# Rounds of weight sums issued by GpSimd instead of SyncE, and two more raw buffers for the first layer's seven block products

## The chip, the cores and the metric

The kernel runs on one core of one Trainium2 chip. The metric is the device time of one execution, in microseconds (us). The core's engines are TensorE (PE, with its weight loads shown as PEld), VectorE (DVE), ScalarE (ACT), GpSimd (POOL) and SyncE (SP). Each works through its own instructions in program order and waits on semaphores for the others. SP only issues DMAs here, and a DMA that has to wait holds back all that stands behind it on the engine that issues it.

## The reference

The network is a trunk of four residual layers on x of shape (256, 1024), float32: layers 0 and 3 are gated MLPs with a causal mix over positions, layer 1 is a dilated window attention, layer 2 a pooling mixer.

```
for i in range(DEPTH):                       # DEPTH = 4
    kind, j = i % 3, i // 3
    h = rms_norm(x, norm_gain[i])
    if kind == 0:   y = mixer_a(h, a_w_in[j], a_v_gain[j], a_w_s[j], a_b_s[j], a_w_out[j])
    elif kind == 1: y = mixer_b(...)
    else:           y = mixer_c(...)
    x = x + y

def mixer_a(h, w_in, v_gain, w_s, b_s, w_out):        # w_in 1024 x 6144, w_out 2048 x 1024
    u, v, z = three blocks of h @ w_in, 2048 wide each
    v = rms_norm(v, v_gain)
    mixed = causal 128x128 matrices, per group and chunk, applied to v, plus b_s
    return (u * mixed * silu(z)) @ w_out
```

## The kernel before

All matmuls are done in three passes: each float32 operand is split into a high part (ACT copies it to a type that PE reads at full rate, line 94) and a low part (DVE subtracts, line 97), and `mm3` (lines 89 to 91) adds high x high, high x low and low x high in PSUM.

**Weights as a stream of units.** All weights come from DRAM as units of 128 x 1024 float32 (512 KB), in the order in which PE uses them. A unit is loaded into a raw buffer (line 181, issued by SP), split into a pair w..h, w..l (seven pairs), and used. `split_units` keeps the splits five units (`AHEAD`) ahead of the product that is being written out, and `load_free` issues the load of a later unit at the point of the program where the raw buffer that it takes has been split for the last time. `raw_place` says which buffer a unit takes: one of four buffers `wr`, and from layer 3's blocks on one of six, `wr` x 4, `xs` and `wx`.

**Seven products instead of eight.** Four products (the first half of the output product of layer 0, `("wo", 0)`, and three pairs of layer 3, `("zu", 0)`, `("zu", 2)`, `("zu", 3)`) are done as 2 x 2 blocks with seven block products instead of eight. For this, sums of weight blocks and sums of blocks of the left operand are needed. `sums_of_quarters` makes the first kind in 32 rounds of 256 columns (`parts`: eight for each of the four products, in the order of `BLOCKS`). A round loads four quarter pieces into `stage` or into the buffer `xs` (512 KB, line 195), adds them in place with four DVE instructions of 128 x 256 (line 198), and writes four sums to a DRAM buffer `sums...` (512 KB, line 201). The units that hold such sums are later loaded from there. In the trace the rounds in `xs` are named `qswo` and `qszu`. `left_sums` makes the second kind on DVE and ACT (lines 592 to 615); in layer 0 it uses the two halves of `wx` and one more tile as room.

**The order of the work.** The program is written out by generators. `tick` moves a clock in program order, one step for every half unit or so; a generator that yields n goes on n ticks later. So the numbers in `sums_of_quarters` (delay before the first round, `load` ticks between the load and the first add, one tick between adds, `wait` ticks more before the write, four ticks to the next load) place the instructions of a round between the others. The queue of each engine is in that order.

In layer 0 the program writes out v (4 x 4 units), then z and u in turn (8 x 4 units, each u followed by a gating step on DVE, lines 759 and 764, and transposes `yp` on PE), then `proj_seven`: seven block products (`xw`, `yw`, `zw`, `xw`, `zw`, `xw`, `ww`) of 12 matmuls and two units each, units 48 to 61. Every product but the first use of a bank adds to what the bank holds, after DVE has added the bank to x (line 636). Then `proj_out` does the rest of the output product, units 62 to 69 (`wo`), line 560 completes x, and layer 1's norm begins: ms on DVE, a power on POOL (line 306), xs on DVE (line 314), transposes on PE, hT on ACT and DVE.

The rounds before: eight for wo0 and four for zu0 in layer 0 (`PARTS = (8, 4, 8, 8)`: one series of eight in `stage` from tick 8, one of four in `xs` from tick 15), sixteen in layer 1, and four in layer 2. POOL has few instructions besides: constants, the powers, the loads of small tables (lines 668 to 671, 902 to 908, 1172, 1174) and memsets in layer 2.

Of the kernel before, what the change touches and what calls it, by code (L numbers as in the profile page):

```python
# [41 lines left out]
MIX_LAG = 4  # L42
LAST_LAG = 1
LAST_AHEAD = 3
WARM = 17
FILL = 4


BLOCKS = {("wo", 0): 48, ("zu", 0): -48, ("zu", 2): -32, ("zu", 3): -16}
PARTS = (8, 4, 8, 8)  # L50


@with_exitstack
def hybrid_trunk_kernel(ctx, tc, x, wts, norm_gainT, a_v_gain, a_wsT, a_bsT, b_gl, b_gv, c_scaleT,
                        masks, rope, rcnt, out):
    nc = tc.nc
# [9 lines left out]
    wx = cp.tile([P, 2, HALF], F32, name="wx")  # L66
# [39 lines left out]
    def spawn(gen, delay=0):  # L106
        if delay == 0:
            try:
                delay = next(gen)
            except StopIteration:  # L110
                return
        tasks.append([now[0] + delay, gen])
# [34 lines left out]
    sums = {(b, j): dp.tile([4, P, UNIT], F32, name=f"sums{b[0]}{b[1]}{j}") for b in BLOCKS for j in range(2)}  # L147

    def first_of(b):

        return BLOCKS[b] % n_units

    for b in sorted(BLOCKS, key=first_of, reverse=True):
        z = first_of(b)
# [3 lines left out]
    n_seq = len(seq)  # L158

    more_raw = seq.index((("zu", 0), 0, 0))  # L160

    raw_users = {"wr": [-1] * RAW_BUFS, "xs": [-1], "wx": [-1]}

    def raw_place(i):

        return ("wr", "wr", "wr", "wr", "xs", "wx")[(i - more_raw) % 6] if i >= more_raw else "wr"

    def load_free():

# [12 lines left out]
            raws.append(raw)  # L182
            loaded[0] += 1

    def sums_of_quarters(parts, shared=False, delay=0, wait=2, load=7):

        if delay:
            yield delay  # L190
        for b, j, c in parts:
            z = first_of(b) + j
            cs = slice(c * 256, (c + 1) * 256)
            q = cp.tile([P, 4, 256], F32, tag="xs", name=f"qs{b[0]}{b[1]}{j}{c}", bufs=1) if shared else stage
            nc.sync.dma_start(q, wts[z:z + 8:2][:, :, cs].rearrange("i p c -> p i c"))
            yield load
            for a, d in ((0, 2), (2, 3), (3, 0), (1, 3)):
                nc.vector.tensor_tensor(q[:, a], q[:, a], q[:, d], op=ALU.add)  # L198
                yield 1
            yield wait  # L200
            nc.sync.dma_start(sums[b, j][:, :, cs].rearrange("i p c -> p i c"), q)
            yield 4

    def split_hi(n):
# [86 lines left out]

    keep_warm(WARM)

# [291 lines left out]
    def left_sums(name, quarter, place, smh, sml, key, pause=1):  # L585

        def full(k, t):
            d = place(f"sq{name}{k}{t}").rearrange("p (k c) -> p k c", c=P)  # L590
            hh, hl = (a.bitcast(F32) for a in quarter(k, t))
            nc.vector.tensor_tensor(d, hh, hl, op=ALU.add)
            return d

        def parted(i, d):
            hi_of(smh[:, i], d)
            yield pause
            lo_of(sml[:, i], d, smh[:, i])
            yield pause

        a22 = full(1, 1)
        yield pause
        a21 = full(0, 1)
        yield pause
        nc.vector.tensor_tensor(a22, a21, a22, op=ALU.subtract)
        yield from parted(S_A21_A22, a22)
        a11 = full(0, 0)
        yield pause
        nc.vector.tensor_tensor(a21, a11, a21, op=ALU.subtract)
        yield from parted(S_A11_A21, a21)  # L610
        nc.vector.tensor_tensor(a11, a22, a11, op=ALU.subtract)
        yield from parted(S_REST, a11)
        a12 = full(1, 0)
        yield pause
        nc.vector.tensor_tensor(a12, a12, a11, op=ALU.add)
        yield from parted(S_A12_REST, a12)
        done.add(key)
# [13 lines left out]
    def proj_seven(layer, yT, smh, sml):  # L631


        def add(t, n, o, op=ALU.add):
            xh = xt[t][:, n * HALF:(n + 1) * HALF]
            nc.vector.tensor_tensor(xh, xh, o, op=op)
            yield 1

        def quarter(k, t):
            return lambda i: yT(4 * k + i, t)  # L640

        xb = pp(f"xw{layer}")
        part_product(xb, quarter(0, 0), True)
        spawn(add(0, 0, xb), 1)
        yb = pp(f"yw{layer}")
        part_product(yb, quarter(1, 0), True)
        spawn(add(0, 0, yb), 1)
        need(("sums", layer))
        zb = pp(f"zw{layer}")
        part_product(zb, sum_tile(smh, sml, S_A21_A22), True)  # L650
        spawn(add(1, 1, zb), 1)
        part_product(xb, sum_tile(smh, sml, S_REST), False)
        spawn(add(0, 1, xb, ALU.subtract), 1)
        part_product(zb, sum_tile(smh, sml, S_A12_REST), False)
        spawn(add(0, 1, zb), 1)
        part_product(xb, sum_tile(smh, sml, S_A11_A21), False)
        spawn(add(1, 1, xb, ALU.subtract), 1)
        spawn(add(1, 0, xb), 1)
        wb = pp(f"ww{layer}")
        part_product(wb, quarter(1, 1), True)  # L660
        spawn(add(1, 0, wb), 1)
# [16 lines left out]
    def layer_a(layer, consts, pl, mid):  # L678
# [101 lines left out]
        if layer == DEPTH - 1 or ("wo", layer) in BLOCKS:  # L780
            smh, sml = pair(pl, [P, 4, 4, P], "sm", f"sm{layer}", 1)
# [65 lines left out]
        for n in range(4):  # L847
            spawn(v_task(n, first if first and n == 0 else
                         proj_tok(f"v{layer}{n}", skew=layer if n == 0 else None)))
            if layer == 0 and n == 0:  # L850
                spawn(sums_of_quarters(parts[:4] + parts[8:8 + PARTS[1]], False, 8, 1, 6))
                spawn(sums_of_quarters(parts[4:8], True, 15, 1, 6))
            if layer == DEPTH - 1 and n == 0:
                spawn(left_sums(layer, h_quarter, lambda n: tmp("sz", n, 4), smh, sml, ("sums", layer)), 4)
        def get(k, t):
# [4 lines left out]
        def y_sums():  # L860

            while ("y", layer, 1) not in done:
                yield 1
            room = [wx[:, 0], wx[:, 1], tmp("yq", "yq", 1)]
            turns = [0]

            def place(name):
                turns[0] += 1
                return room[(turns[0] - 1) % 3]

            def y_quarter(k, t):
                return (a[:, :, t * P:(t + 1) * P] for a in yT[k])

            yield from left_sums(layer, y_quarter, place, smh, sml, ("sums", layer), 2)

        for n in range(4):
            if n == 2 and ("wo", layer) in BLOCKS:
# [14 lines left out]

        if ("wo", layer) in BLOCKS:
            proj_seven(layer, get, smh, sml)
        proj_out(layer, 16, get, KT if layer == DEPTH - 1 or ("wo", layer) in BLOCKS else 0)


# [21 lines left out]
    def layer_b(layer, consts, pl):  # L919
# [215 lines left out]
        for hp in range(NHEAD // 2):  # L1135
            for g in range(NG):
                spawn(qk_task(hp, g, proj_tok(f"qk{hp}{g}", skew=layer if hp == 0 and g == 0 else None)))
                if hp == 0 and g == 0:
                    n0, n1, n2 = (sum(PARTS[:i]) for i in (2, 3, 4))
                    spawn(sums_of_quarters(parts[n0:n1]))  # L1140
# [28 lines left out]
    def layer_c(layer, pl):  # L1169
# [103 lines left out]

        a, b, c, d = C_ORDER
        spawn(gate_tok(a, proj_tok(f"cz{a}", skew=layer)))
        spawn(sums_of_quarters(parts[sum(PARTS):], wait=8))
        spawn(gate_feat(b, proj_feat(f"cz{b}")))
        spawn(pool_task(a, proj_feat(f"cx{a}")))
        spawn(pool_task(b, proj_feat(f"cx{b}")))
# [19 lines left out]
    parts = [(b, j, c) for b in BLOCKS for j in range(2) for c in range(4)]  # L1299
# [157 lines left out]
```

## Time and profile before

| | |
|---|---|
| median of 3 runs | 841.59 us (839.37 to 841.69) |
| the profiled execution, its own time | 840.14 us |
| its span, first to last instruction | 838.4 us |
| busy PE, DVE, ACT, POOL | 823.8, 640.8, 523.4, 43.8 us |
| mean granted TensorE clock | 0.995 of full speed |
| DMA | 195.75 MB, mean 233 GB/s |

The span and the time of the profiled execution differ by 1.74 us, which lie around the instructions. Busy time of PE is an upper bound: matmuls overlap, and a matmul at half the clock counts as busy too.

### The profile page before, as it was taken

What the parts mean: (1) busy time and instruction counts of PE and PEld (TensorE: products, weight loads), DVE (VectorE), ACT (ScalarE), POOL (GpSimd) and SP (SyncE); (2) the same over time, 40 slices, a digit from 0 to 9 for tenths busy, and PEclk for the clock granted to TensorE, in tenths of its full rate; (3) what the DMA queues carried; (4) which work ended last, traced back from release to release, by engine and by line L of the source; (5) the groups of instructions that cost most, each with busy time, mean ns of one, the idle gap of its engine ahead of it and who ended that gap; (6) DMA issues with size and microseconds to landing.
All of it is one profiled execution on the core that took longest, in us unless ns stands there. A gap on an engine that the chain in (4) does not pass through costs nothing.

```text
span 838.4 us, 12737 instructions
## 1 busy us (share of the span) xinstructions
PE 823.8 (98%) x4573; PEld 710.1 (85%) x4573; DVE 640.8 (76%) x1112; ACT 523.4 (62%) x957; POOL 43.8 (5%) x69
## 2 busy tenths in 40 slices
PE   9999999889999999999999999999999999999998
PEld 7887888668988988988988989999988888788887
DVE  5797788876858768768768676798964799979692
ACT  7675454454858778678678557445643659657570
POOL 1101000000001001001001012000000000000000
PEclk9999999989999999999999999999999999999999
DMA  8889886694796767757656258656696258868661
GB/s 290 308 286 322 295 295 209 232 303 161 268 330 207 224 205 237 235 184 248 224 193 224 86 176 295 213 193 211 211 316 221 97 185 305 306 200 318 213 260 51
DMA packets 79424, 195.75 MB, mean 233 GB/s; under 512 B 6304, under 2 KB 39856, under 8 KB 79232
## 3 DMA queue, kind: packets, MB, share of 16 engines
q1 hardware_dynamic: 78096, 190.86, 67.3%
q0 software_dynamic: 976, 3.79, 1.4%
q8 instruction: 36, 0.59, 0.3%
q10 hardware_dynamic: 288, 0.28, 0.2%
q14 instruction: 28, 0.23, 0.1%
HBM read 177.08 MB, written 17.83 MB: 232 GB/s over the span
## 4 chain that ended last, share of the span: by engine, by line
PE 80%; DVE 8%; DMA 6%; ACT 3%; issue 3%; POOL 0%; ACTq 0%; DVEq 0%
PE qk L91 5%; PE qk L89 5%; PE qk L90 5%; DMA wr<-in_wts_dram 5%; PE wo L89 4%; PE wo L91 4%; PE wo L90 4%; PE v L89 2%; PE v L91 2%; PE v L90 2%; PE cz L91 2%; PE cz L89 2%; PE cz L90 2%; PE cx L89 2%; PE cx L90 2%
## 5 line engine op out<-in xcount | busy, mean ns | idle before, releaser
L198 DVE TENSOR_TENSOR stage<-stage 128x256 f32<-128x256 f32 x80 | 33.5, 419 | 2.4 <-DMA stage<-in_wts_dram 1.9
L942 POOL TENSOR_TENSOR qr<-qm,m 128x8 f32<-128x8 f32 x12 | 20.1, 1675 | 228.7 <-DVE qm L941 228.7
L937 ACT ACTIVATE junk<-qk 128x128 bf16<-128x128 f32 x96 | 26.7, 278 | 7.3 <-PE qk L91 4.6
L946 ACT ACTIVATE qn<-qk,qr 128x128 f32<-128x128 f32 x96 | 27.6, 382 | 3.6 <-POOL qr L942 3.6
L324 ACT ACTIVATE hT<-hp,gT 128x128 fp32r<-128x128 f32 x48 | 13.1, 383 | 14.9 <-PE hp L320 14.9
L560 DVE TENSOR_TENSOR x<-wo,x 128x512 f32<-128x512 f32 (+1 forms) x16 | 10.8, 673 | 13.3 <-PE wo L91 13.3
L941 DVE TENSOR_SCALAR qm<-qs 128x8 f32<-128x8 f32 x12 | 2.1, 172 | 22.1 <-ACT junk L937 22.1
L306 POOL TENSOR_TENSOR r<-ms,m 128x1 f32<-128x1 f32 x6 | 4.3, 710 | 280.6 <-DVE ms L303 280.6
L937 ACT ACTIVATION_READ_ACCUMULATOR junk<-qk 128x1 f32 x96 | 18.8, 196 | 0.0
L329 DVE SCALAR_TENSOR_TENSOR hT<-hp,gT,hT 128x128 fp32r<-128x128 f32 x48 | 13.5, 343 | 6.2 <-ACT hT L324 6.2
L298 ACT ACTIVATE junk<-x 128x512 bf16<-128x512 f32 x16 | 10.2, 638 | 10.1 <-DVE x L560 9.9
L1036 ACT ACTIVATE p<-p,rl 128x384 f32<-128x384 f32 (+1 forms) x16 | 11.5, 769 | 6.1 <-DVE rl L1035 6.1
L967 PE MATMUL qt<-ident,qn 128*128 128x128 f32 x96 | 14.5, 274 | 0.4 <-DVE qk00l L975 0.4
L967 PEld LDWEIGHTS qt<-ident,qn 128*128 128x128 f32 x96 | 11.3, 140 | 3.7 <-issue 1.9
L198 DVE TENSOR_TENSOR qszu<-qszu 128x256 f32<-128x256 f32 x32 | 13.4, 420 | 0.4 <-DMA qszu<-in_wts_dram 0.2
L959 DVE TENSOR_TENSOR rb<-qn,kcb 128x32 f32<-128x32 f32 x96 | 13.7, 183 | 0.0
L1032 ACT ACTIVATE p<-p,nb 128x768 f32<-128x768 f32 x8 | 7.5, 938 | 7.3 <-DVE nb L1031 7.3
L772 PEld LDWEIGHTS yp<-ident,yy 128*128 128x128 f32 x64 | 7.5, 139 | 5.3 <-issue 1.4
L772 PE MATMUL yp<-ident,yy 128*128 128x128 f32 x64 | 9.9, 277 | 2.0 <-DVE yy L764 1.0
L955 DVE TENSOR_TENSOR ra<-qn,kcb 128x64 f32<-128x64 f32 x48 | 10.5, 220 | 0.8
L697 DVE TENSOR_TENSOR vv<-v,kc 128x512 f32<-128x512 f32 x16 | 10.3, 682 | 0.7 <-ACT junk L695 0.7
L759 DVE SCALAR_TENSOR_TENSOR sz<-u,m,sz 128x512 f32<-128x512 f32 x8 | 6.0, 745 | 5.3 <-PE u L91 5.3
(3030 smaller groups left out, 3377.3 us busy)
## 6 DMA issues: line engine op xcount, KB each, us to landing
wr<-in_wts_dram SPq DMA_DIRECT2D x256, 512.0 KB, 4.6
stage<-in_wts_dram SPq DMA_DIRECT2D x20, 512.0 KB, 5.1
wr<-sumszu SPq DMA_DIRECT2D x20, 512.0 KB, 4.6
sumszu<-stage SPq DMA_DIRECT2D x16, 512.0 KB, 6.2
wr<-sumswo SPq DMA_DIRECT2D x8, 512.0 KB, 4.6
qszu<-in_wts_dram SPq DMA_DIRECT2D x8, 512.0 KB, 5.0
sumszu<-qszu SPq DMA_DIRECT2D x8, 512.0 KB, 5.0
wx<-in_wts_dram SPq DMA_DIRECT2D x7, 512.0 KB, 5.6
```

The source lines that it names most:

```text
L89: nc.tensor.matmul(out_ap, lh[0], rh[0], start=start, stop=False, skip_group_check=True)
L90: nc.tensor.matmul(out_ap, lh[0], rh[1], start=False, stop=False, skip_group_check=True)
L91: nc.tensor.matmul(out_ap, lh[1], rh[0], start=False, stop=stop, skip_group_check=True)
L198: nc.vector.tensor_tensor(q[:, a], q[:, a], q[:, d], op=ALU.add)
L324: nc.scalar.activation(h_parts(layer)[0][:, k, t * P:(t + 1) * P], pt[:, k % 4], AF.Copy, scale=gT[:, layer, k:k + 1])
L329: nc.vector.scalar_tensor_tensor(hTl, pt[:, k % 4], gT[:, layer, k:k + 1], hTh.bitcast(F32), op0=ALU.mult, op1=ALU.subtract)
L772: nc.tensor.transpose(pt[:, k], ys[t][:, k * P:(k + 1) * P], ident)
L937: nc.scalar.activation(junk[:, :HD], ov[t][:, h], AF.Square, accum_out=ssq[t][:, h:h + 1])
L942: nc.gpsimd.tensor_tensor(rqs, ms, m05_row[:, :8], op=ALU.pow)
L946: nc.scalar.activation(qn[t][:, h], ov[t][:, h], AF.Copy, scale=rq[t][:, h:h + 1])
L959: nc.vector.tensor_tensor(rb[:, hs, s0:s0 + 16], qn[t][:, hs, s1:s1 + 16], c, op=ALU.mult)
L967: nc.tensor.transpose(pts[t][:, h], qn[t][:, h], ident)
```

## The change

The rounds of layers 0 and 2 are issued by GpSimd (`queue=nc.gpsimd`), loads and writes alike; those of layer 1 stay on SP. Layer 0's eight rounds for wo0 are dealt to `stage` and `xs` in turn (four each, from tick 4 and tick 11). The rounds for zu0 that stood behind them in layer 0 go from four to two, and these two begin after `proj_seven` has been written out. Layer 1 has sixteen rounds as before, layer 2 has six instead of four, each 19 ticks after the last instead of 23. The 14 units of the first layer's seven products take six raw buffers, with `xs` and `wx` at the fifth and sixth place. `left_sums` in layer 0 pauses one tick between its steps instead of two.

```
+MORE = 2
-PARTS = (8, 4, 8, 8)
+PARTS = (8, 2, 8, 8)
...
     more_raw = seq.index((("zu", 0), 0, 0))
+    out_raw = first_of(("wo", 0))
...
     def raw_place(i):
-        return ("wr", "wr", "wr", "wr", "xs", "wx")[(i - more_raw) % 6] if i >= more_raw else "wr"
+        six = i >= more_raw or out_raw <= i < out_raw + 14
+        return ("xs", "wx", "wr", "wr", "wr", "wr")[(i - (more_raw if i >= more_raw else out_raw) + MORE) % 6] if six else "wr"
...
-    def sums_of_quarters(parts, shared=False, delay=0, wait=2, load=7):
+    def sums_of_quarters(parts, shared=False, delay=0, wait=2, load=7, queue=nc.sync):
...
-            nc.sync.dma_start(q, wts[z:z + 8:2][:, :, cs].rearrange("i p c -> p i c"))
+            queue.dma_start(q, wts[z:z + 8:2][:, :, cs].rearrange("i p c -> p i c"))
...
-            nc.sync.dma_start(sums[b, j][:, :, cs].rearrange("i p c -> p i c"), q)
+            queue.dma_start(sums[b, j][:, :, cs].rearrange("i p c -> p i c"), q)
...
-                spawn(sums_of_quarters(parts[:4] + parts[8:8 + PARTS[1]], False, 8, 1, 6))
-                spawn(sums_of_quarters(parts[4:8], True, 15, 1, 6))
+                spawn(sums_of_quarters(parts[0:8:2], False, 4, 1, 6, nc.gpsimd))
+                spawn(sums_of_quarters(parts[1:8:2], True, 11, 1, 6, nc.gpsimd))
...
-            yield from left_sums(layer, y_quarter, place, smh, sml, ("sums", layer), 2)
+            yield from left_sums(layer, y_quarter, place, smh, sml, ("sums", layer))
...
             proj_seven(layer, get, smh, sml)
+            spawn(sums_of_quarters(parts[8:8 + PARTS[1]], False, 0, 1, 5, nc.gpsimd))
...
-        spawn(sums_of_quarters(parts[sum(PARTS):], wait=8))
+        spawn(sums_of_quarters(parts[sum(PARTS):], False, 0, 4, 7, nc.gpsimd))
```

## Rows read from the trace of the kernel before

**Rows 1.** Stretches of 5 us: busy time of each engine, granted clock, DMA share, GB/s

```profile
150.00:155.00 5.00, 5.00 (x26) 4.12 (x24) 4.96 (x9) 2.95 (x4) 0.00 (x0) 1.00 0.14 36
...
180.00:185.00 5.00, 4.97 (x12) 3.90 (x13) 4.81 (x7) 2.81 (x3) 0.00 (x0) 0.50 0.84 261
```

**Rows 2.** Timeline of PE: start, duration, instruction, idle before and its releaser

```profile
78.71 0.74 PE L772 MATMUL yp<-ident,yy 128*128 128x128 f32 x4 [1.02 <-DVE yy L764]
...
149.52 0.39 PE L89 MATMUL xw<-w48h,y00h 128*128 128x512 f32 x1
...
152.24 0.60 PE L772 MATMUL yp<-ident,yy 128*128 128x128 f32 x4
...
156.20 0.66 PE L772 MATMUL yp<-ident,yy 128*128 128x128 f32 x4 [0.59 <-DVE y03l L97]
...
163.56 0.47 PE L89 MATMUL zw<-w56h,sm0h 128*128 128x512 f32 x1 [1.22 <-DVE x L636]
...
166.95 0.47 PE L89 MATMUL xw<-w58h,sm0h 128*128 128x512 f32 x1 [0.42 <-DVE x L636]
...
176.53 0.47 PE L89 MATMUL wo<-w63h,y02h 128*128 128x512 f32 x1 [1.10 <-DVE x L636]
...
180.03 0.79 PE L89 MATMUL wo<-w63h,y02h 128*128 128x512 f32 x1 [2.56 <-DVE x L636]
...
190.12 0.39 PE L89 MATMUL wo<-w66h,y03h 128*128 128x512 f32 x1
```

**Rows 3.** Chain of work that ended last, 140 to 200 us: start, duration, what

```profile
159.37 4.41 DMA wr<-sumswo
```

**Rows 4.** Timeline of SP's DMA issues, merged: start, duration with waits, DMA, count

```profile
145.36 8.74 SPq L181 DMA_DIRECT2D wr<-in_wts_dram  x2
155.24 6.79 SPq L181 DMA_DIRECT2D wr<-sumswo  x4
```

**Rows 5.** Timeline of DVE in the seven products, and one row of 65 us

```profile
65.64 1.22 DVE L97 TENSOR_TENSOR w24l<-wr,w24h 128x1024 fp32r<-128x1024 f32 x1
...
149.04 0.75 DVE L759 SCALAR_TENSOR_TENSOR sz<-u,m,sz 128x512 f32<-128x512 f32 x1 [3.71 <-PE u L91]
...
152.19 0.42 DVE L198 TENSOR_TENSOR stage<-stage 128x256 f32<-128x256 f32 x1
152.52 1.22 DVE L97 TENSOR_TENSOR w53l<-wr,w53h 128x1024 fp32r<-128x1024 f32 x1
153.65 0.42 DVE L198 TENSOR_TENSOR stage<-stage 128x256 f32<-128x256 f32 x1
...
162.73 0.68 DVE L636 TENSOR_TENSOR x<-x,zw 128x512 f32<-128x512 f32 x1
163.33 1.22 DVE L97 TENSOR_TENSOR w59l<-wr,w59h 128x1024 fp32r<-128x1024 f32 x1
```

**Rows 6.** Waits of SP's queue: total us, times, longest

```profile
SPq L195 <- DMA sumszu<-stage: 15.5, 6, 4.0
```

**Rows 7.** Groups and timeline of POOL: its DMA issues (busy total, mean ns)

```profile
L669 POOL DMA_DIRECT2D kc<-in_a_wsT_dram x2 | 1.3, 650 | 0.0
...
65.69 0.61 POOL L902 DMA_DIRECT2D kcb<-in_b_gl_dram  x1 [5.03 <-DVE wsr01l L727]
```

**Rows 8.** DMA issues by line: count, KB each, median us from issue to landing

```profile
wr<-in_wts_dram SPq DMA_DIRECT2D x256, 512.0 KB, 4.6
stage<-in_wts_dram SPq DMA_DIRECT2D x20, 512.0 KB, 5.1
...
sumswo<-stage SPq DMA_DIRECT2D x4, 512.0 KB, 7.5
...
kc<-in_a_wsT_dram POOLq DMA_DIRECT2D x2, 512.0 KB, 7.9
```

**Rows 9.** Stretches of 50 us: the first layer's z and u products

```profile
50.00:100.00 50.00, 48.87 (x230) 40.33 (x229) 39.32 (x61) 28.19 (x33) 4.25 (x8) 1.00 0.90 305
```

**Rows 10.** Timeline of DVE where layer 2 ends and layer 3 begins

```profile
658.87 0.87 DVE L314 TENSOR_SCALAR xs<-x,r 128x512 f32<-128x512 f32 x2
```

## What was predicted

> **What bounds the kernel now.** I read the table of the profiled execution first: PE is busy nearly all of the span, so a gain has to come from places where PE waits or runs at half clock. The stretches of 5 us show the one large place: around the first layer's seven products PE's count in 180 to 185 us falls to 12 matmuls at a granted clock of 0.50, the lower level (1.2 of 2.4 GHz), and at 150 to 155 us DMA moves only 36 GB/s, just ahead of the time when the loads are needed [rows 1]. Elsewhere the 5 us stretches up to 260 us are full but for about a microsecond near 79 us [rows 2].
>
> The timeline of PE gives the size. The first product starts at 149.52, the next work after it at 152.24: 2.72 us for a product of 12 matmuls. From 149.52 to 190.12 PE does seven products and four units of the rest, each unit also 12 matmuls: 11 x 2.72 = 29.9 us, with two groups of transposes of at most 0.6 us each 31.1. It takes 40.6. So 9.5 us are lost: five waits of 0.59, 1.22, 0.42, 1.10 and 2.56 us, the slow stretch after the last, and the restarts [rows 2].
>
> The chain says why: a load of sums stands in it with 4.41 us, later one of weights likewise, with DVE and ACT between [rows 3]. SP's timeline shows the first cause: of the two loads issued from 145.36 the second ended its wait 8.74 us later, and those of the four following units with sums came from 155.24 on [rows 4]. The second is unit 57, which takes the raw buffer of unit 53; DVE gets to unit 53's low part at 152.52, behind a gating step of 3.15 us (149.04 to 152.19) that itself waits for PE, and behind a round's add [rows 5]. So raw buffers are given back late, loads start late, and splits, adds to x and PE follow.
>
> **The change, part by part.**
>
> *Six buffers.* By the code's order unit 57 now takes unit 51's buffer, 58 takes 52's, 59 takes 53's. Units 51 and 52 were split before the gating step, so 57 and 58 can be issued before 149 instead of up to and after 155.24 [rows 4]. From unit 64 on the four `wr` serve alone again, so 64 still waits for 60's low part.
>
> *No rounds beside them.* Two rounds' adds stood there, and each costs DVE 0.33 us by the next start (152.19 to 152.52) [rows 5]: 1.3 us ahead of the first two waits, 1.3 near the last.
>
> *What is left.* With the loads early, DVE's own list sets the pace. Prices by start to start: gating 3.15, split 1.13 (152.52 to 153.65), add to x 0.60 (162.73 to 163.33); the low part of y, the same size, 0.60 [rows 5]. A product needs two splits and an add, 2.86 us, against PE's 2.72. I add up DVE in program order from 149.04. The add that frees bank `zw` for the fifth product ends after gating, six splits, two low parts of y and three adds: 149.04 + 3.15 + 6.78 + 1.20 + 1.80 = 161.97. PE gets there at 149.52 + 4 x 2.72 + 0.7 to 1.2 = 161.1 to 161.6: a wait of 0.4 to 0.9. Next, two splits and an add: 164.83, against PE at about 164.7: 0.1. The next bank needs four splits and three adds more: 171.15, PE at 170.3: 0.9. Then unit 64: its buffer is free after unit 60's low part (164.23); 4.6 us to land [rows 8], about 1 on ACT, ready at 169.9, where DVE would take it at 168.8: 1.1 to 1.5 late. So 1.4 to 3.4 us of 9.5 stay, no wait is as long as the 2.56 that stood before the slow stretch [rows 2], and the gain is 6.1 to 8.1. **I take 7.0.**
>
> *Left operand's sums at one tick a step.* The same twelve DVE instructions, of 0.60 by size, come in half the time, while z and u of the third block run. There DVE is busy 39.3 of 50 us [rows 9], so room is 10.7 us in 50, about 3.5 in these 16; some 3.6 us of the twelve are moved in. It just fits; what is late is the next gating step and PE's transposes behind it, which already waited 1.02 us once for DVE [rows 2]. Bounds: 1.0 lost, or 1.3 gained if that wait and another of 0.3 go. The second needs SP to be ahead, which is what the next part gives. I take +0.3.
>
> *Issue by GpSimd.* SP issued a round's load only when the buffer's last write had landed, and all weight loads stood behind it: 15.5 us in six waits for one kind [rows 6]. That goes in layers 0 and 2, but has value only where PE waits, so it is within the term above. The Trainium skill, "DMA: Bandwidth & Descriptors", section "Issuing engines are not separate DMA queues", says that DMAs run on the same 16 engines whoever issues them, and that another issuer saves only the time to initiate them. The waits of SP's queue disagree in so far as they show waiting, not initiating; by the page this term would be 0 and the sum 5.9.
>
> On POOL a DMA of 128 runs is busy 0.65 us [rows 7]; a round's has 512 runs (four pieces of 1 KB in 128 partitions), which no row shows. Bounds: 0.65 (by the DMA) to 2.6 (by the run). I take the lower third, about 1. POOL is nearly idle, so its time costs nothing; what counts is the chain of one series. From a round's last add to the next round's first add there are 12 ticks in layer 0, of 1.36 us (two to a product): 16.3 us. In them lie two issues, a write (7.5) and a load (5.1) [rows 8]: 12.6 + 2 x 0.65 to 2 x 2.6 = 13.9 to 17.8. With the one POOL landing of 512 KB, 7.9 [rows 8], in place of both: 17.1 to 21.0. At my value it fits; the ends return as a rival. POOL's instructions behind a waiting DMA are the powers for v and for layer 1's norm and the loads of layer 1's tables; the order of ticks puts a load four ticks after the write that it waits for, so a power can be held by 7.5 - 5.4 = 2 us, ahead of work on ACT and DVE that is five units ahead of PE. Cost 0.
>
> *The two rounds behind the products.* The tenth round's adds stay in the norm that begins layer 1, and its write comes two ticks later than the last write of layer 0 did. Layer 1's first round on SP waits for that write, with weight loads behind it. Cost 0 to 2.8 us (a landing of 7.9 instead of 5.1 [rows 8], passed on in full); I take 0.8, since raw buffers are full there.
>
> *Two more rounds in layer 2.* The waits of PE have none in that layer now. By the ticks the sixth round's adds fall on the last tail ticks and the norm of layer 3, two of them ahead of the xs at 658.87, which is on time to a fraction of a microsecond [rows 10]. Cost 0 to 4 x 0.33 = 1.3; I take 0.3, as DVE has short gaps before it.
>
> **Sum.** 7.0 + 0.3 - 0.8 - 0.3 = 6.2 us. The profiled execution took 840.14 (span 838.4), so 833.9; the median shown is 1.45 above it: 841.6 - 6.2 = **835.4**. Its bounds: 6.1 - 1.0 - 2.8 - 1.3 = 1.0 and 8.1 + 1.3 = 9.4, that is 832.2 to 840.6. Under 0.3% (2.5 us) a difference can hardly be told from none here.
>
> **Rivals.**
>
> *More goes than I think* (0.08): DVE's list is overtaken because splits run ahead before 149 us and no wait stays: 9.5 + 1.3 less 0.3, about 831. For it: the low DMA rate at 150 to 155 us is gone and DVE was idle for 3.71 us before the gating step [rows 1, 5]. Against: AHEAD is still five units.
>
> *DVE becomes the bound* (0.12): the waits come back as waits on the adds to x, since a product costs DVE 2.86 and PE 2.72, and the pressed left sums add a backlog. Two waits of 2 us near each other and the slow clock again would leave a gain of about 2: 839.6. For it: all five waits already end on DVE [rows 2].
>
> *It does not do what it says* (0.05): `wx` is held by the left sums when unit 53 wants it, or the sums land so late that SP waits at unit 52; then loads are as late as now: 841.6. Against: by the ticks both are done four to eight ticks before.
>
> *Slower* (0.11): GpSimd's chain doesn't fit. At 21.0 us in 16.3 each of the six rounds that follow another in layer 0 makes DVE wait up to 4.7 us, 28 in all, over some 82 us in which DVE has about 17.5 free [rows 9]: 10.5 reach PE, 841.6 - 6.2 + 10.5 = 845.9. It decides against the change from a chain of about 20.7 us on, which is 4.4 late a round. For it: the POOL landing of 7.9 and the unknown issue. The Trainium skill, "SBUF — State Buffer", section "SBUF: two separate sides", warns that GpSimd can't write descriptors while VectorE runs an instruction in a two-port mode. Against it is the issue at 65.69 of 0.61 us, like the 0.65 of the others [rows 7], while DVE was at work on a split from 65.64 on [rows 5]; if it held, each issue would wait out up to one split, 1.2 us, twice a round, and the chain would still fit at the lower landings.
>
> **Chances.** The forecast has 0.64. Faster by over 0.3%: 0.61 of the forecast, all of "more goes" (0.08) and 0.05 of "DVE": 0.74. Slower: 0.11. The same: the rest, 0.15. The range 831 to 841 leaves out the slower rival, half of the one that does nothing and some of "more goes", about 0.17.
>
> **What would show it.** Right: no wait of PE over 1.5 us and a clock of 1.00 from the first product to the tail; that stretch some 7 us shorter; DMA rate at the first product far above 36 GB/s; round loads on POOL issued right after the write's landing; PE full in layer 2. Wrong: DVE waiting for `stage` or `qs` loads in the first layer, issues of over 2 us on POOL, SP waiting at the loads into `xs` or `wx`, a PE wait at the start of layer 1, or a clock of 0.5 in a stretch that was full.

## Result: 844.7 us, slower by 0.43%, and the profile after

The changed kernel takes 844.67 us (median of 20 runs, 837.89 to 849.86), the kernel before 840.08 (20 runs beside them, 838.32 to 843.51): a ratio of 1.0043 with a 95% interval of 1.0022 to 1.0063. 835.4 was predicted, and 831 to 841 as the range. The profiled execution was one of the quicker: 842.22 us, span 840.5, 2.1 longer than the span before.

The gain was there, and was lost elsewhere. The table gives the start of the first matmul of some units, from the timelines of PE, and the differences that the text uses:

| | before | after | change |
|---|---|---|---|
| unit 24 (third block of z and u) | 74.8 | 75.1 | +0.3 |
| from 24 to 28 | 13.5 | 19.5 | +6.0 |
| from 28 to 48 | 61.2 | 61.0 | -0.2 |
| from 48 to 66 (seven products and what follows) | 40.6 | 33.0 | -7.6 |
| from 66 to 74 | 23.7 | 23.7 | 0.0 |
| from 74 to 82 (start of layer 1) | 23.2 | 26.5 | +3.3 |
| from 82 to the end of the span | 601.4 | 601.7 | +0.3 |
| span | 838.4 | 840.5 | +2.1 |

**The products.** Stretches of 5 us of the changed kernel (PE, PEld, DVE, ACT and POOL busy, granted clock, DMA share, GB/s); the products start at 155.57:

```profile
150.00:155.00 5.00, 5.00 (x25) 4.16 (x24) 1.19 (x1) 1.06 (x1) 0.00 (x0) 1.00 0.82 294
155.00:160.00 5.00, 5.00 (x26) 4.16 (x25) 4.83 (x8) 2.13 (x3) 0.00 (x0) 1.00 0.00 0
...
180.00:185.00 5.00, 4.24 (x19) 3.30 (x18) 4.73 (x7) 2.75 (x3) 0.00 (x0) 1.00 0.88 279
```

Just before the products the loads now run at 294 GB/s, and the clock is 1.00 in all stretches from 150 to 190 us (0.50 after the last product in [rows 1]). In the stretch in which the products start, 155 to 160, nothing is moved, less even than the 36 GB/s of [rows 1], and PE has no wait there: the loads issued so far, up to unit 58, have landed. Its timeline of PE has two waits left from 155.57 to 188.63, where [rows 2] had five:

```profile
168.27 0.47 PE L90 MATMUL zw<-w56h,sm0h 128*128 128x512 f32 x1 [0.69 <-DVE x L639]
...
181.02 0.50 PE L90 MATMUL wo<-w63h,y02h 128*128 128x512 f32 x1 [0.76 <-DVE x L639]
```

Its timeline of SP shows what six buffers did. Units 52 to 55 (sums), 56 and 57 (weights) and 58 (sums) were issued from 141.36 to 151.22, before the gating step that starts on DVE at 155.09; the kernel before ended the wait of unit 57 only at about 154, behind the start of its step (149.04), and issued 58 at 155.24 [rows 4]. The three loads of sums behind it, units 59 to 61, still come after the step, from 159.48 on.

```profile
141.36 0.33 SPq L184 DMA_DIRECT2D wr<-sumswo  x1
141.80 0.37 SPq L184 DMA_DIRECT2D wx<-sumswo  x1
142.26 4.42 SPq L184 DMA_DIRECT2D wr<-sumswo  x2
147.49 1.47 SPq L184 DMA_DIRECT2D wr<-in_wts_dram  x2
151.22 0.33 SPq L184 DMA_DIRECT2D wr<-sumswo  x1
159.48 0.33 SPq L184 DMA_DIRECT2D wx<-sumswo  x1
160.62 2.65 SPq L184 DMA_DIRECT2D wr<-sumswo  x2
```

In the chain that ended last no load of sums stands in this part ([rows 3] had one of 4.41 us), only a load of weights of 4.44 at 175.03.

**The first loss.** The timeline of PE has one new large wait, at the transposes of the third block:

```profile
83.42 1.09 PE L775 MATMUL yp<-ident,yy 128*128 128x128 f32 x4 [5.42 <-DVE yy L767]
```

It is the wait of 1.02 us in [rows 2], grown to 5.42. The chain that ended last tells where it is from (start, duration, what):

```profile
66.69 1.29 DVE wsr01l L730
...
68.27 0.56 POOL kcb L906
...
70.41 10.10 DMA stage<-in_wts_dram
...
82.09 0.67 DVE sz L762
...
82.79 0.50 DVE yy L767
...
83.42 1.09 PE yp L775 x4
```

A load of 512 KB for a round takes 10.10 us, right behind the loads of layer 1's tables. In the timeline of DVE, the first add of this round stands in program order right ahead of a split and the gating step, and waits:

```profile
80.53 0.43 DVE L201 TENSOR_TENSOR stage<-stage 128x256 f32<-128x256 f32 x1 [5.88 <-DMA stage<-in_wts_dram]
80.88 1.22 DVE L98 TENSOR_TENSOR w28l<-wr,w28h 128x1024 fp32r<-128x1024 f32 x1
82.01 0.75 DVE L762 SCALAR_TENSOR_TENSOR sz<-u,m,sz 128x512 f32<-128x512 f32 x1
```

The add is not alone in holding the gating step. The split between the two, of unit 28, needs ACT's high part of that unit, and this was late as well (timelines of DVE and ACT):

```profile
57.55 0.89 DVE L201 TENSOR_TENSOR stage<-stage 128x256 f32<-128x256 f32 x2 [2.10 <-DMA stage<-in_wts_dram]
...
77.87 1.06 ACT L95 ACTIVATE w28h<-wr 128x1024 fp32r<-128x1024 f32 x1 [5.19 <-DMA wr<-in_wts_dram]
```

In the kernel before (chain that ended last, and timelines of ACT and DVE):

```profile
66.89 8.07 DMA wr<-in_wts_dram
...
75.06 1.06 ACT L94 ACTIVATE w28h<-wr 128x1024 fp32r<-128x1024 f32 x1 [2.77 <-PE u L91]
...
77.30 0.74 DVE L759 SCALAR_TENSOR_TENSOR sz<-u,m,sz 128x512 f32<-128x512 f32 x1
```

The step comes 4.7 us later than before (82.01 against 77.30). Unit 28's high part was done at 78.93; with no add in front, its split would have started there and not at 80.88. So the add of the third round holds the step for 1.95 us. The other 2.8 come with unit 28's own load. It was issued at 69.47 in place of 66.89, when the split of unit 24 had freed its buffer, and took 8.4 us until ACT began. DVE was late with that split, after it had waited 2.10 us for the round before; in e9 below, where that wait was 0.32, it split unit 24 at 65.85, here at 68.22.

Stretches of 5 us of the same kernel show the price:

```profile
70.00:75.00 5.00, 5.00 (x24) 4.12 (x23) 4.07 (x5) 2.68 (x3) 1.94 (x3) 1.00 0.93 247
75.00:80.00 5.00, 3.01 (x14) 2.16 (x12) 0.00 (x0) 1.06 (x1) 0.00 (x0) 1.00 1.00 379
80.00:85.00 5.00, 1.58 (x6) 1.47 (x7) 4.39 (x8) 1.51 (x2) 0.75 (x1) 0.59 0.76 271
```

DVE does nothing from 75 to 80, PE stands still for 5.4 us, and the granted clock is 0.59 from 80 to 85, in which it starts again; PE runs part of unit 25 at the lower level. While the tables are loaded, the DMA engines are busy for 0.93 of the time and move 247 GB/s; just after it, 379.

**The second loss.** At the start of layer 1 the timeline of PE has this wait, again with matmuls at the lower clock behind it:

```profile
227.15 0.65 PE L971 MATMUL qt<-ident,qn 128*128 128x128 f32 x4 [1.97 <-DVE qk00l L979]
```

The chain that ended last, in the same stretch:

```profile
211.07 5.89 DMA sumszu<-stage
...
217.03 0.38 SPq L198
...
217.50 5.96 DMA wr<-in_wts_dram
...
223.56 1.07 ACT w81h L95
...
225.80 0.42 DVE stage L201
...
226.53 0.49 DVE qk00l L979
...
227.15 0.65 PE qt L971 x4
```

GpSimd issues the tenth round's write at 211.07; SP's load of the next round, at 217.03, waits for its landing; unit 81's load stands behind that on SP, and all that follows is late. The size is that of one profile: six more kernels below leave this place and its issuer as they are, and from 74 to 82 they take 24.0 to 26.7 us.

**The issue.** A group of POOL in a list of all lines of the changed kernel (busy, mean ns, idle before), and DMA issues from its page (count, KB each, median us to landing):

```profile
L198 POOL DMA_DIRECT2D stage<-in_wts_dram x12 | 9.2, 766 | 34.4 <-DMA sumszu<-stage 22.6 <-DMA sumswo<-stage 11.8
```

```profile
stage<-in_wts_dram POOLq DMA_DIRECT2D x12, 512.0 KB, 6.7
sumszu<-stage POOLq DMA_DIRECT2D x8, 512.0 KB, 5.6
stage<-in_wts_dram SPq DMA_DIRECT2D x8, 512.0 KB, 5.0
```

A round's DMA keeps POOL for 0.77 us, near the 0.65 of [rows 7]. Its load lands in 6.7 us by the median, where SP's take 5.0 ([rows 8]: 5.1).

### The profile page after: what moved, and what is told of

Same layout as the page of the kernel before. It is cut to its first block, busy times and chain, and to the rows that moved or that the text cites. A ratio compares the mean times of both kernels' runs of the same rounds, so it can differ in the third digit from the quotient of the medians.

```text
span 840.5 us, 12759 instructions
## 1 busy us (share of the span) xinstructions
PE 824.4 (98%) x4573; PEld 712.4 (85%) x4573; DVE 641.8 (76%) x1112; ACT 523.2 (62%) x957; POOL 67.4 (8%) x101
## 4 chain that ended last, share of the span: by engine, by line
PE 77%; DVE 8%; DMA 7%; issue 4%; ACT 3%; POOL 1%; SPq 0%; DVEq 0%; ACTq 0%; POOLq 0%
PE qk L92 5%; PE qk L90 5%; PE qk L91 5%; PE wo L90 4%; PE wo L92 4%; PE wo L91 4%; DMA wr<-in_wts_dram 3%; PE v L90 2%; PE v L92 2%; PE v L91 2%; DMA stage<-in_wts_dram 2%; PE cz L91 2%; PE cz L90 2%; PE cx L91 2%; PE cz L92 2%
## 5 line engine op out<-in xcount | busy, mean ns | idle before, releaser
L563 DVE TENSOR_TENSOR x<-wo,x 128x512 f32<-128x512 f32 (+1 forms) x16 | 10.8, 673 | 13.4 <-PE wo L92 13.3
L332 DVE SCALAR_TENSOR_TENSOR hT<-hp,gT,hT 128x128 fp32r<-128x128 f32 x48 | 13.5, 344 | 5.8 <-ACT hT L327 5.8
L204 POOL DMA_DIRECT2D sumszu<-stage x8 | 6.1, 768 | 141.3 <-DVE stage L201 141.3
L301 ACT ACTIVATE junk<-x 128x512 bf16<-128x512 f32 x16 | 10.2, 639 | 10.1 <-DVE x L563 9.9
L963 DVE TENSOR_TENSOR rb<-qn,kcb 128x32 f32<-128x32 f32 x96 | 13.9, 187 | 0.0
L201 DVE TENSOR_TENSOR qszu<-qszu 128x256 f32<-128x256 f32 x32 | 13.4, 420 | 0.5 <-DMA qszu<-in_wts_dram 0.3
L198 POOL DMA_DIRECT2D stage<-in_wts_dram x12 | 9.2, 766 | 34.4 <-DMA sumszu<-stage 22.6
```

The source lines that it names most:

```text
L332: nc.vector.scalar_tensor_tensor(hTl, pt[:, k % 4], gT[:, layer, k:k + 1], hTh.bitcast(F32), op0=ALU.mult, op1=ALU.subtract)
L963: nc.vector.tensor_tensor(rb[:, hs, s0:s0 + 16], qn[t][:, hs, s1:s1 + 16], c, op=ALU.mult)
```

## The experiments

Each ratio is against the kernel before on the same chip. "A" marks a change to the changed kernel, "B" one to the kernel before. The marks are all from the timelines of PE (us), of the one profile that each kernel has; e7 and e13, whose programs don't differ up to unit 28, are 2.4 us apart between 24 and 28.

| run | 24 to 28 | 48 to 66 | 74 to 82 | median | ratio, 95% interval |
|---|---|---|---|---|---|
| changed kernel | 19.5 | 33.0 | 26.5 | 844.67 | 1.0043 [1.0022, 1.0063] |
| e1_all_sync | 18.2 | 33.0 | 28.0 | 842.40 | 1.0044 [1.0024, 1.0064] |
| e2_first_sync | 17.3 | 33.0 | 24.0 | 839.66 | 0.9995 [0.9978, 1.0013] |
| e5_two_issuers | 20.2 | 33.4 | 25.0 | 844.59 | 1.0054 [1.0024, 1.0083] |
| e4_queue_only | 12.7 | 38.1 | 22.7 | 838.71 | 0.9986 [0.9970, 1.0003] |
| e6_tables_later | 11.8 | 33.6 | 24.4 | 836.93 | 0.9987 [0.9956, 1.0019] |
| e7_old_ticks | 13.4 | 33.0 | 25.6 | 836.49 | 0.9959 [0.9942, 0.9977] |
| e8_layer1_later | 19.4 | 33.3 | 22.8 | 843.78 | 1.0037 [1.0009, 1.0065] |
| e9_both_later | 11.8 | 33.0 | 22.8 | 838.05 | 0.9986 [0.9964, 1.0008] |
| e10_old_ticks_layer1 | 14.2 | 33.2 | 22.8 | 835.57 | 0.9950 [0.9932, 0.9967] |
| e11_old_ticks_sync | 12.3 | 32.8 | 24.8 | 834.04 | 0.9941 [0.9920, 0.9963] |
| e12_four_buffers | 13.7 | 37.9 | 26.7 | 839.30 | 0.9983 [0.9964, 1.0002] |
| e13_rounds_beside | 15.8 | 35.6 | 22.9 | 836.79 | 0.9968 [0.9954, 0.9982] |

**Is it the issuer?** My first theory was that GpSimd's queue (tables, powers and rounds one behind the other) made the round late. e1_all_sync (A) gives all rounds back to SP, at the new places:

```
-    parts[0:8:2], False, 4, 1, 6, nc.gpsimd      parts[1:8:2], True, 11, 1, 6, nc.gpsimd
+    parts[0:8:2], False, 4, 1, 6, nc.sync        parts[1:8:2], True, 11, 1, 6, nc.sync
     (the two rounds behind the products and layer 2's likewise)
```

> All rounds of the changed kernel go back to SP; places, buffers and counts stay as changed. Theory (GpSimd's single queue, in which a load of one series waits for its landing ahead of the write of the other series, makes the third stage load late and DVE with it): the 5.4 us wait of PE at the first transposes of y goes to 1.5 us or less, unit 24 to unit 28 takes 13.5 to 14.5 us instead of 19.5, the seven products and the four units after them keep their gain (33 to 34 us instead of 40.6), and the whole takes 833 to 837 us, ratio to before 0.992 to 0.997. Rival (the new places of the rounds, with adds on the gating step's ticks, cost it, whoever issues): the wait stays at 3 us or more and the whole at 840 or more.

The theory fell. The ratio is 1.0044, DVE waits at the same add before the same gating step, as its timeline shows, and PE waits 3.56 us at the transposes. Here the add's own share is only 0.7: unit 28's high part was done at 78.03, and its split began at 78.77.

```profile
78.43 0.42 DVE L201 TENSOR_TENSOR stage<-stage 128x256 f32<-128x256 f32 x1 [4.76 <-DMA stage<-in_wts_dram]
...
79.91 0.74 DVE L762 SCALAR_TENSOR_TENSOR sz<-u,m,sz 128x512 f32<-128x512 f32 x1
```

e2_first_sync (A) gives SP only the two series that start at ticks 4 and 11; e5_two_issuers (A) only the one in `xs`:

```
 e2: parts[0:8:2], False, 4, 1, 6, nc.sync      parts[1:8:2], True, 11, 1, 6, nc.sync
 e5: parts[1:8:2], True, 11, 1, 6, nc.sync
```

> Only the two series beside v, z and u of the first layer go back to SP; the two rounds behind the products and those of layer 2 stay on GpSimd. Theory: as with all rounds on SP in the first 190 us (wait at y's transposes 1.5 us or less), and the loss of some 3 us at the start of layer 1 stays: 835 to 839 us, 0 to 3 us more than with all on SP. Rival (layer 2 or the rounds behind the products carry the loss of the median): 842 or more.

> The changed kernel with one of the two series of the first layer, that in xs, issued by SP; that in stage stays on GpSimd. No write of one series now stands behind a load of the other. Theory (interlock of two series in one queue): the late third stage load is gone, it is issued within 8 us after the second's write and DVE waits less than 2 us for it; 835 to 839 us. Rival (DMAs issued by GpSimd land late by themselves): DVE still waits 4 us or more for stage loads, which take 8 to 10 us to land, and the whole is 840 or more.

With SP for the first layer's series the time is that of the kernel before, with the loss at 24 to 28 a little smaller (17.3) and still there. So at the new places the issuer does count: 0.9995 against 1.0043, with intervals that do not touch. DVE waited 0.62, 1.15 and 4.91 us for the first three rounds in `stage`, in the changed kernel 1.71, 2.10 and 5.88. And e1, which differs from e2 only in that SP also issues the two rounds behind the products and those of layer 2, is slower again, with 28.0 from 74 to 82 where e2 has 24.0. With one series each the time is that of the changed kernel, and a new loss stands ahead of unit 24 (79.2 against 75.1), to which e8 comes back. e4_queue_only (B) moves the issue alone, at the old places:

```
+    ..., queue=nc.sync):        # and queue.dma_start in the two places
-    spawn(sums_of_quarters(parts[:4] + parts[8:8 + PARTS[1]], False, 8, 1, 6))
+    spawn(sums_of_quarters(parts[:4] + parts[8:8 + PARTS[1]], False, 8, 1, 6, nc.gpsimd))
     (and the series in xs and in layer 2 likewise)
```

> The kernel before, with nothing changed but the issuer: GpSimd for the rounds of layers 0 and 2. Places, buffers, counts as before. Theory: the two series interlock in GpSimd's queue here too, so DVE waits 5 us or more in all for the rounds' loads in the first layer (4.5 before), and the products lose what they lost before or more, since the last rounds run late beside them: 844 to 852 us, ratio 1.005 to 1.015. Rival (places cost it, not the issuer): 839 to 842 us, ratio within 0.002 of 1.

No loss at 24 to 28, and in its one profile 2.5 us less in the products, where four buffers still serve. So at the old places GpSimd as the issuer costs nothing; the loss comes with the new ones, and there it is larger with GpSimd.

**Is it the places?** e6_tables_later (A) moves only the loads of layer 1's tables, twelve ticks later. e7_old_ticks (A) moves only the two series, back to the ticks of before:

```
 e6: -spawn(load_b())                              +spawn(load_b(), 12)
 e7: -parts[0:8:2], False, 4, 1, 6, nc.gpsimd      +parts[0:8:2], False, 8, 1, 6, nc.gpsimd
     -parts[1:8:2], True, 11, 1, 6, nc.gpsimd      +parts[1:8:2], True, 15, 1, 6, nc.gpsimd
```

> The changed kernel with layer 1's four table loads started 12 ticks later. New theory (the places of the rounds, not the issuer: the third stage round's load goes out right behind the table loads, lands some 10 us after, and its first add stands in DVE's order just before the gating step): the third stage load lands within 7 us, DVE waits for it 1 us or less and PE 1.5 us or less at the first transposes of y; unit 24 to 28 takes 13.5 to 15 us instead of 19.5; the whole 837 to 840 us. Rival (it is the adds' position alone, or the doubled series of DMAs in one queue): PE waits 3 us or more there and the whole stays at 843 or more.

> The changed kernel with the two series of the first layer begun at tick 8 and 15, as before, instead of 4 and 11; all else as changed, GpSimd included. New theory (places): with the third round's adds at ticks 44 to 47, behind the gating step of tick 40, a late load no longer holds that step; unit 24 to 28 takes 13 to 14.5 us, the whole 836 to 839.5 us. Rival (the crowd of DMAs at that time holds up unit 28's own load, whichever round is where): ACT waits 3 us or more for unit 28 and the whole stays at 842 or more.

Each alone takes the whole first loss away: from 24 to 48 e6 takes 74.8 us and e7 75.0, the kernel before 74.7, the changed kernel 80.5 (in e6 2.0 of what 24 to 28 gains is lost again by 48, where the tables are now). In e6 the round stands where it stood in the changed kernel, and its load, with no tables beside it, lands in time, as unit 28's does (high part from 71.55); DVE and the gating step go on (timelines of POOL and of DVE):

```profile
67.38 0.76 POOL L198 DMA_DIRECT2D stage<-in_wts_dram  x1 [4.40 <-DMA sumswo<-stage]
```

```profile
72.90 0.43 DVE L201 TENSOR_TENSOR stage<-stage 128x256 f32<-128x256 f32 x1 [0.27 <-DMA stage<-in_wts_dram]
...
74.40 0.75 DVE L762 SCALAR_TENSOR_TENSOR sz<-u,m,sz 128x512 f32<-128x512 f32 x1
```

That is 5.5 us from issue to add, against 10.1. In e7 the round's late load still makes DVE wait, but after the gating step, where it costs nothing; for unit 28's high part DVE still waited 3.21 us, 2.27 in the kernel before, and PE's wait is 0.98 (timeline of DVE):

```profile
77.61 0.74 DVE L762 SCALAR_TENSOR_TENSOR sz<-u,m,sz 128x512 f32<-128x512 f32 x1
...
79.19 0.74 DVE L762 SCALAR_TENSOR_TENSOR sz<-u,m,sz 128x512 f32<-128x512 f32 x1
...
85.43 0.42 DVE L201 TENSOR_TENSOR stage<-stage 128x256 f32<-128x256 f32 x1 [2.86 <-DMA stage<-in_wts_dram]
```

e7 is faster than the kernel before, and its five runs lie within 1.8 us (835.87 to 837.70); the ten of e6 go from 834.3 to 845.3. So something else still hangs on tick 4 or 11.

**Layer 1, and a second place.** e8_layer1_later (A) starts layer 1's rounds six ticks later, e9_both_later has this and e6's edit:

```
-    spawn(sums_of_quarters(parts[n0:n1]))
+    spawn(sums_of_quarters(parts[n0:n1], delay=6))
```

> The changed kernel with layer 1's first series of rounds, on SP, begun six ticks later. Theory (SP waits at that series' first load until the tenth round's write has landed, and unit 81's load stands behind it): ACT waits 1 us or less for unit 81 instead of 2.3, unit 74 to unit 82 takes 22.7 to 23.3 us instead of 26.5, the whole 2 to 3.5 us less than the changed kernel: 841 to 843. Rival (the two rounds' adds on DVE in the norm cost it): 74 to 82 stays above 25.5.

> Both: table loads 12 ticks later and layer 1's first series six ticks later. Theory: the two losses add up, so both gains do: 834 to 837.5 us, ratio to before 0.993 to 0.997, with the seven products' stretch (unit 48 to 66) still at 33 to 34 us. Rival: less than 2 us below the kernel before.

From unit 74 to 82 both take 22.8 us: the second loss is the wait for the tenth round's write, and it goes with six ticks. In the medians that does not show: 1.0037 against 1.0043 for the changed kernel, 0.9986 (e9) against 0.9987 (e6). e8's profile starts unit 24 at 81.1, 6 us late. Its timelines of POOL and DVE show the second place that the early ticks touch:

```profile
28.52 5.04 POOL L677 TENSOR_SCALAR_AFFINE_SELECT kc<-kc 128x128 f32<-128x128 f32 x8 [7.62 <-DMA kc<-in_a_wsT_dram]
33.50 0.79 POOL L198 DMA_DIRECT2D stage<-in_wts_dram  x1
```

```profile
34.55 1.27 DVE L700 TENSOR_TENSOR vv<-v,kc 128x512 f32<-128x512 f32 x2
41.91 0.43 DVE L201 TENSOR_TENSOR stage<-stage 128x256 f32<-128x256 f32 x1 [6.09 <-DMA stage<-in_wts_dram]
```

POOL's selects of the mixing matrices stand ahead of the first load. They took 5.04 us here, 2.01 in the profile of the changed kernel, where DVE waited 1.71 for the same round, and 6.05 in that of e5, where it waited 5.59. In e10 they took 3.98 and DVE didn't wait, since the adds stand four ticks later. So a round at tick 4 issued by GpSimd has so little lead that it is late in some executions. The spread of the runs fits: from the quickest to the slowest it is 9.2 to 12.1 us in the five kernels with GpSimd at tick 4 (the changed kernel, e5, e6, e8, e9), 6.0 in both with SP there (e1, e2), and 1.8 to 5.9 in all at the old ticks. That late selects make the slow runs was not shown: e9's profiled execution is its quickest (832.51), and its slow ones, up to 842.35, left no trace.

**The rest of the change, at the old ticks.** e10 is e7 with e8's edit; e11 is e7 with the two series on SP; e12 is e7 with four raw buffers in layer 0; e13 is e7 with two rounds beside the products and none behind.

```
 e10: spawn(sums_of_quarters(parts[n0:n1], delay=6))
 e11: sums_of_quarters(parts[0:8:2], False, 8, 1, 6)      sums_of_quarters(parts[1:8:2], True, 15, 1, 6)
 e12: six = i >= more_raw
 e13: PARTS = (8, 4, 8, 8)
      sums_of_quarters(parts[0:8:2] + parts[8:8 + PARTS[1]], False, 8, 1, 6, nc.gpsimd)
      (without the spawn behind proj_seven)
```

> The changed kernel with two places put otherwise: the first layer's two series start at ticks 8 and 15, as before, and layer 1's series six ticks later. My theory (the places cost, the issuer doesn't) expects both losses gone: first matmul with unit 24 at about 75, with unit 28 at 88 to 89 (94.6 in the changed kernel), the stretch from unit 48 to unit 66 at 33 us (33.0 in the changed kernel, 40.6 before), from unit 74 to unit 82 at 22.8 (26.5 in the changed kernel), and the time at 836.5 less 2 to 3, so 833 to 835, with runs within 2 us of each other. The rival, that the two places only pass the loss on (raw buffers are full, so PE waits elsewhere), expects 74 to 82 at 25 or a new wait in layer 1, and 836 to 837.

> The changed kernel with the first layer's two series at ticks 8 and 15 and issued by SP, the two rounds behind the products and the third layer's still by GpSimd. It isolates the issuer where the places are good. If the issuer is worth nothing, 836 to 837 and the same marks as with GpSimd at these ticks (unit 28 at 88.6, unit 48 at 150.2, 48 to 66 at 33.0). If GpSimd's issue is needed for the gain in the products (SP is held at a round's load and the loads behind it start late), 48 to 66 goes back towards 36 to 38 and the time to 839 to 841, with SP waiting for writes of sums in layer 0.

> The changed kernel with the series at ticks 8 and 15, and without the two more raw buffers of the first layer (four serve there, as before). It isolates the buffers from the absence of rounds. If the buffers carry most of the 7 us, 48 to 66 takes 38 to 40 us (33.0 with six), unit 57's load is again issued only after 152, and the time is 841 to 843. If the rounds that no longer stand beside the products carry it, 48 to 66 takes 34 to 36 and the time is 838 to 839. By the prices on record, two adds at 0.33 us ahead of each wait, the rounds' share would be 1.3 us of each of two waits, so 37 to 38 and about 841.

> The changed kernel with the series at ticks 8 and 15 and six buffers, but with the two rounds back in the first series, so that they stand beside the products as before; none stands behind them, and the third layer has four rounds as before. If the buffers carry the 7 us alone, 48 to 66 stays at 33 to 34 us, and 74 to 82 falls to 23 since the tenth round's write comes early: 833 to 835. If DVE has no room for the rounds beside the products, 48 to 66 takes 35 to 38 us, with waits of PE for adds and splits there, and the time is 836 to 839.

e10 beats both kernels: 835.57 (834.81 to 837.09), 0.9950 of the kernel before. The stretch from 74 to 82 falls to 22.8 as expected, but from 82 on it takes 602.7 where e7 takes 601.8, so the rounds moved later return 0.9 of the 2.8, and 24 to 28 took 14.2 against 13.4. Of the two theories neither is quite right: the place is mended, part of it comes back. The ratios of e10 and e7 (0.9950 and 0.9959) can't be told apart.

e11 is as fast, 834.04 (0.9941, an interval that overlaps those of e7 and e10), with 32.8 us in the products: at these ticks and with six buffers the issuer doesn't matter. Its timeline of SP shows round DMAs between the weight loads, with no hold that PE feels.

e12 and e13 split the gain. Four buffers without the rounds give 37.9, six with the rounds beside the products 35.6, six without 33.0. So without the rounds two more buffers are worth 4.9 us, and with six buffers the absence of the rounds is worth 2.6. The fourth corner, four buffers with the rounds beside, was measured twice: 40.6 in the kernel before (issue by SP), 38.1 in e4 (by GpSimd, as in e12 and e13). From the first the parts are 5.0 and 2.7 and add up to 7.6. From the second, which also keeps the old dealing of the rounds, they are 2.5 and 0.2 and don't add up. So what the absence of the rounds is worth with four buffers stays open; each of these numbers is from one profile. With four buffers the last four loads of sums (units 58 to 61) are again issued only after the gating step, which starts at 149.66 (timeline of SP in e12):

```profile
145.78 8.60 SPq L184 DMA_DIRECT2D wr<-in_wts_dram  x2
155.19 6.12 SPq L184 DMA_DIRECT2D wr<-sumswo  x4
```

In e13, where the tenth round's write comes early, 74 to 82 takes 22.9 without any delay in layer 1, which confirms the cause of the second loss from another side. From 24 to 28 it takes 15.8 at the old ticks: DVE waits 3.45 us for unit 28's high part, and PE 2.01 at the transposes. So unit 28's late load alone, with no round in front, can cost some 2 us there.

## Why the prediction was wrong

**What was right.** The products: 7.0 predicted within 6.1 to 8.1, 7.6 measured. DVE's list sets the pace there in the main as worked out: 0.4 to 0.9 was foretold for the fifth product and 0.69 came, in all 1.4 to 3.4, and two waits of 1.45 came. The second is in another place than foretold: no wait came at the next bank (0.9) or for unit 64 (1.1 to 1.5), but 0.76 for a later add to x, behind units 65 and 66. The rounds' adds were priced at 1.3 us ahead of the first two waits and 1.3 near the last, 2.6, and e13 against e7 gives 2.6; with four buffers the price is 2.7 or 0.2, by the corner that is taken. The sign "DMA rate at the first product far above 36 GB/s" did not come: the rate there is 0, as the loads issued by then had landed. Three of the five signs of "Wrong" came: DVE waited for `stage` in the first layer, PE at the start of layer 1, and the clock fell in stretches that were full. A round's DMA on POOL costs 0.77 us (about 1 taken). Layer 2's two rounds: from unit 164 to 214 both kernels take 138.1 us, and the xs that answers to [rows 10] comes without a wait, at 660.98. The rounds' adds stand right before it:

```profile
660.65 0.42 DVE L201 TENSOR_TENSOR stage<-stage 128x256 f32<-128x256 f32 x1
660.98 0.88 DVE L317 TENSOR_SCALAR xs<-x,r 128x512 f32<-128x512 f32 x2
```

The left operand's sums at one tick cost nothing that shows: 28 to 48 takes 61.0 against 61.2.

**The step that failed** is "Issue by GpSimd", in the place where it says "Cost 0" and "At my value it fits". It took the landings of [rows 8], with the issues 13.9 to 17.8 us, or 17.1 to 21.0 with POOL's landing, against 16.3 us for the 12 ticks of a series, and had no term for where the new starts, ticks 4 and 11 in place of 8 and 15, put a round. For the third round in `stage` the chain measured: the last add of the round before ended at 61.95, the write was issued at 64.20 (behind the powers for v), the next load at 70.41 (behind four tables), landed 10.1 us later, at 80.5. That is 18.6 us; DVE got to the add at 74.65, so 12.7 were there and not 16.3. The gating step stood behind this add and behind unit 28's split. It came 4.7 us late, 1.95 of them by this add and 2.8 by unit 28's load, which started late after DVE's wait for the round before; so PE's wait at the transposes grew from 1.02 to 5.42, and the lower clock made that a loss of 6.0. I had named what is behind a waiting DMA on POOL (the powers and tables), but not what is behind the waiting adds on DVE: the gating step, and the splits that give raw buffers back. e7 puts the price of the ticks alone at 0.9959 against 1.0043, 0.84% or 7.1 us, which is more than the predicted gain.

The rival "slower: GpSimd's chain doesn't fit" (0.11) had the sign and nearly the time, 845.9, but by luck: one round and not six is late by 5.9, two others by 1.7 and 2.1, and e1 shows that the third is late by 4.8 with SP as well. At these places the issuer has a part (e2), which no one run takes to pieces. The Trainium skill, "DMA: Bandwidth & Descriptors", section "Issuing engines are not separate DMA queues", says that another issuer saves only the time to initiate DMAs: by it the term is about 0, and e11 beside e7 agrees (32.8 against 33.0 us in the products). At ticks 4 and 11 e2 beside the changed kernel does not (0.9995 against 1.0043). Where raw buffers are short, e4's profile differs: the products took 2.5 us less with the issue by GpSimd alone. That SP's waits no longer hold the weight loads does not explain it: SP issues units 56 to 61 at the same distance from the first product as before (from 4.2 us ahead, the sums from 5.7 behind). The cause is open, and one profile each does not exclude chance. An issue held up by VectorE, as weighed among the rivals, didn't show: in the first layer's z and u each of a round's issues on POOL took 0.75 to 0.80 us beside DVE at work.

**"The two rounds behind the products"** had the right mechanism and the wrong size: 0.8 taken, 2.8 as the bound, 3.3 measured in this profile, 0.8 to 3.5 in the seven that leave the place and its issuer as they are. The write landed in 5.9 us, not in 7.9; what the term lacked is the wait of PE itself with the lower clock behind it. e8 and e13 confirm the cause.

**The sum.** In the profiled executions: 7.6 gained in the products and 0.2 by unit 48, against 6.0, 3.3, 0.3 and 0.3: 2.1 lost. The medians differ by more (4.6) since the changed kernel's runs reach from 838 to 850; one place that makes some of them long is shown in e8, and how often it is hit is open. A version with e6's, e8's and e11's edits at the old ticks was not run.

## What to carry to other kernels

When work is dealt anew or started earlier, price each place where a wait may now stand: write down what is behind it on the engine that waits (here an add of no urgency stood ahead of a gating step that PE needs), and which transfers run at that time. The place decides the price of a wait: 2.9 us after the gating step cost nothing. And ask what else the work behind it is waiting for: of 5.9 us ahead of the gating step only 1.95 went into it, since a weight load that it also needs was late at the same time. A large gain can hide its loss: the marks of a few units along the program, before against after, show both at once, and each part is then worth undoing by itself.

## What was not expected of the hardware

Small tables slow large loads by more than their bytes: while 835 KB of tables (192, 576, 64 and 3 KB) were loaded, a load of 512 KB took 10.1 us, in e6 without them 5.5, with the DMA engines busy 0.93 of the time at 247 GB/s. At the 379 GB/s that came just after, 835 KB would take about 2.2 us (an estimate). In e6, where the tables come later, it is a weight load beside them that takes 8.73 us. No run here separates the size of their pieces from their number. The same eight selects on POOL took 2.01 us in one profiled execution, 5.04 in another and 6.05 in a third, so a DMA issued behind them can't be given a fixed time.
